# The gate rows of the second PEER layer: a new layout for one operand, and ScalarE for every second group of the other

## The chip, the core and the metric

The kernel runs on one core of a Trainium2 chip. The metric is the device time of one execution in microseconds (us). A core has a matrix engine (TensorE, "PE" in the rows; its weight loads are "PEld"), three engines that work elementwise (VectorE "DVE", ScalarE "ACT", GpSimd "POOL"), and 16 DMA engines that are fed from queues, those of SyncE ("SPq") and GpSimd ("POOLq") here. Every engine takes its instructions in the order in which they stand in its queue; semaphores order engines among each other. That order was fixed when the program was built: a scheduler goes through the instructions in the order in which the code emits them, and lets a later instruction of an engine go ahead of an earlier one that by its own reckoning isn't ready yet.

## What is computed

Two layers of a trunk, each of a mixer and a PEER feed-forward. Only the second PEER (layer 1, no context output: 512 tokens, four tiles of 128) is touched:

```python
q = (hb @ w_q).reshape(PEER_BLOCK, PEER_HEADS, 2, half)
s = jnp.einsum('nhpd,pkd->nhpk', q, sub_keys)
sv, si = lax.top_k(s, PEER_TOPK)
...
top_s, pos = lax.top_k(cand, PEER_TOPK)      # 16 of the pairs (i, j) for each of 8 heads
gate = jax.nn.softmax(top_s, axis=-1)
act = gelu(einsum('nd,nhkd->nhk', hb, u_tab[eidx]))
w = gate * act
out = einsum('nhk,nhkd->nd', w, v_tab[eidx])
```

Each token picks 8 x 16 = 128 experts out of 128 x 128, an expert being a pair (i, j) with a gate.

## The kernel before

The second PEER is `peer_streams`. It treats its four token tiles in two ways. Two of them (`gath`) are gathered: for each of 128 slots of a tile an indirect DMA brings one row of 8 KB for each token (`gather`: POOL issues it, DVE multiplies and sums the first half against the token, ACT makes the gelu and the weight, DVE adds the second half into `acc`). Two tiles (`dense`, 256 tokens) go through all 16384 experts as matmuls: `u_pair` loads a pair of chunks of `u` (`u_raw`), multiplies it with the 256 tokens, takes the gelu, and keeps the result in a ring of 14 tiles in on-chip memory, or, when the ring is full, stores it to DRAM (`aw`, `A_d`) and loads it back later. Then 64 steps of a second loop load a pair of chunks of `v` (`v_raw`), multiply the activations with the gates (`gg`, on POOL, L1459) and accumulate `res` on TensorE; a step also makes a `u_pair` if any is left, or reloads one from `A_d`.

The gates of the dense tiles must be spread over all experts first, and that is what `build` does: for a token, the 128 x 128 matrix of gates is the product of two matrices whose rows are the token's 128 picks, one with a one at column i (`o1`), one with the gate at column j (`o2`). `tr` holds i (negated), j and the gate with the picks on partitions and the tokens along the free axis; `ib` and `jb` are i and j in bfloat16. A group is W8 = 4 tokens: DVE makes `o1` (compare a counting row with i, L1273), `oe` (compare with j, L1275; the counting row is repeated four times, tokens innermost, which is also how `oe` is laid out) and `o2` (`oe` times the gate, L1276). `o2` is stored token by token, so L1276 walks its output with a stride of 128 elements, and each of the four matmuls (L1281, recorded at the helper's line L73) reads 128 elements that lie side by side. ACT copies the product into `stage` (L1283), and after 16 tokens a DMA stores the stage to `G_d`. Each tile has 32 groups, so there are 64 in all. `o1` and `o2` have two buffers each, `oe` one. In the trace `o1` and `o2` are both called `o`. A float32 matmul is recorded as two passes, so a group is eight records of 128 columns.

The first PEER (`peer`, layer 0) builds its gates by another function of its own, lines 818 to 840: `o1` by ACT (four Abs, L829, and one Relu, L830), `o2` by DVE.

What is emitted when is set by a planner written into the kernel. `fill` is called after each piece of TensorE's work with that work's time. It advances a clock for TensorE and emits pieces of other work until DVE's clock has caught up: pieces of `choice` (selection of the experts of a tile, and `build` of the tile before, in turns), and gather slots, one unit of slot time for three of `choice` (FRONT_SHARE). The times are those of the table PAY. While `choice` lasts, each turn also emits a `u_pair`; when it is used up, the pools of this stage close, and the loop over `v` follows. The slots left over are emitted along that loop and at its end.

Of the kernel before, what the change touches and what calls it, by code (L numbers as in the profile page):

```python
# [9 lines left out]
F32 = mybir.dt.float32  # L10
# [4 lines left out]
AF = mybir.ActivationFunctionType  # L15
OP = mybir.AluOpType
# [64 lines left out]
def kernel(tc, a, out):  # L81
    nc = tc.nc
    V, S, G, PE, SP = nc.vector, nc.scalar, nc.gpsimd, Tracked(nc.tensor), nc.sync
# [7 lines left out]
    def pool(stack, name, bufs=1, space=None, side="left"):  # L91
        return stack.enter_context(tc.tile_pool(name=name, bufs=bufs, space=space, reuse_waits="tile") if space
                                   else tc.tile_pool(name=name, bufs=bufs, side=side, reuse_waits="tile"))
# [9 lines left out]
    def kt(shape, name, dt=F32):  # L103
        return kp.tile(shape, dt, name=name)
# [19 lines left out]
    iota, row = kt([P, P], "iota"), kt([P, 1], "row")  # L124
# [1002 lines left out]
    def peer_streams(op, l, gt, xdst):  # L1127
# [4 lines left out]
        n, nr = nd * P, (nd + ng - 1) * P  # L1132
# [10 lines left out]
        wp = pool(ef, "ps_f")  # L1143
# [3 lines left out]
        iotab = wp.tile([P, P], BF16, name="iotab")  # L1147
# [109 lines left out]
        W8, W4 = 4, 4  # L1257
# [3 lines left out]
        def build(t):  # L1261

            tr, ib, jb = chosen.pop(t)
            for g in range(P // TG):
                stg = wp.tile([P, P, TG], F32, name="stage", bufs=2)
                for b in range(TG // W8):
                    n0 = g * TG + b * W8
                    nb = slice(n0, n0 + W8)
                    sh, hs = [P, W8, P], [P, P, W8]
                    o1 = wp.tile(sh, F32, name="o1", bufs=2)  # L1270
                    oe = wp.tile(hs, BF16, name="oe", bufs=1)
                    o2 = wp.tile(sh, F32, name="o2", bufs=2)
                    V.tensor_tensor(o1, iotab.unsqueeze(1).to_broadcast(sh), ib[:, nb].unsqueeze(2).to_broadcast(sh),  # L1273
                                    op=OP.is_equal)
                    V.tensor_tensor(oe, iotar, jb[:, nb].unsqueeze(1).to_broadcast(hs), op=OP.is_equal)  # L1275
                    V.tensor_tensor(o2.rearrange("p n c -> p c n"), oe, tr[:, 2, nb].unsqueeze(1).to_broadcast(hs),  # L1276
                                    op=OP.mult)
                    for i4 in range(0, W8, W4):
                        pq = pp.tile([P, W4, P], F32, name="gps", tag="misc", bufs=4)
                        for i in range(W4):  # L1280
                            PE.matmul(pq[:, i], o1[:, i4 + i], o2[:, i4 + i], start=True, stop=True)  # L1281
                        n1 = b * W8 + i4
                        S.copy(stg[:, :, n1:n1 + W4].rearrange("p i n -> p n i"), pq)  # L1283
                        yield "build"
                tg = (dense.index(t) * P) // TG + g
                SP.dma_start(G_d[:, :, tg], stg.rearrange("p (q c) m -> p q (c m)", c=GG))

        def gather(i):
# [23 lines left out]
            for args in late:  # L1312
# [1 line left out]

        clock = {"pe": 0.0, "dve": 0.0, "dma": 0.0}
        PAY = {"score": (1.75, 0, .25), "cand": (.6, 0, 0), "top": (.85, 0, 0), "top2": (.55, 0, 0), "decode": (1.0, 0, 0),
               "eq": (1.4, 0, 0), "tree": (1.05, 0, 0), "gates": (1.0, 0, .6), "build": (1.9, .65, .9),
               "slot": (2.75, 2.5, 0)}

        def pay(kind):  # L1320
# [12 lines left out]
        def choice():  # L1333
            yield from select(dense[0])
            for t, u in zip(dense, [*dense[1:], gath[1]]):
                gens = [build(t), select(u)]
                while gens:
                    for q in list(gens):
                        kind = next(q, None)
                        if kind is None:  # L1340
                            gens.remove(q)
                        else:
                            yield kind
# [103 lines left out]
        for j in range(NP):  # L1447
            c = 2 * j
# [561 lines left out]
    with ExitStack() as es:  # L2010
        gt = gather_state(0, es)
        op = mixer0(gt)
        nxt = peer(op, 0, gt, x_d[1])
    with ExitStack() as es:
        gt = gather_state(1, es)
        op = mixer1(*nxt, gt)
        peer_streams(op, 1, gt, out.rearrange("(t p) d -> t p d", p=P))
# [76 lines left out]
```

## Time and profile before

| | us |
|---|---|
| median of 3 runs | 3853.35 |
| lowest and highest of the runs | 3850.56, 3860.54 |
| the profiled execution, its own time | 3857.99 |
| span of the profiled execution | 3856.2 |

A row of instructions gives line, engine, operation, output<-inputs, shapes and count, then busy time in us and mean ns of one, then the engine's idle time just before them and what ended it. A mean ns is the duration of one record; records of TensorE overlap, so its rate is busy time divided by count. [...] The profile's own table of busy shares over the whole span mixes this layer with the first one, and says little about it.

### The profile page before, as it was taken

Reading aid. Unit: us, or ns where it says so; the run is one execution under the profiler, and the core shown is the slowest. Engines: PE = TensorE matmul, PEld = TensorE weight load, DVE = VectorE, ACT = ScalarE, POOL = GpSimd, SP = SyncE. Lnnn points to the kernel's source line nnn. Section 1 sums busy time; section 2 is a strip of 40 time slices with the busy share of each in tenths; the row PEclk is TensorE's granted clock in tenths of the full one; section 3 lists DMA queues with packets and bytes.
Section 4 is the critical chain, followed back from the end, with each engine's and each line's share of the span. In section 5 each row is a group of like instructions: output and inputs, shape, how many; then the busy total and the mean of one; then the engine's idle time right before and its main releaser. Section 6 shows DMA issues by size and latency. Waiting matters only on the chain. (4 is left out here: it accounts for less than half of the span.)

```text
span 3856.2 us, 50097 instructions
## 1 busy us (share of the span) xinstructions
PE 3538.3 (92%) x17628; PEld 2749.2 (71%) x17628; DVE 3009.0 (78%) x6281; ACT 1409.0 (37%) x2760; POOL 1635.1 (42%) x1225
## 2 busy tenths in 40 slices
PE   7789999999999999999998999979998789898987
PEld 6567877788888778888887888755887336555643
DVE  4877899999999868988886616469999556766675
ACT  4243322378888933322224424312343111111110
POOL 3300055446444557888771203101123344545462
PEclk8899999999999999999999999899999899999988
DMA  5225588889999999999994330245699999999995
GB/s 231 88 85 191 178 325 308 308 313 358 359 346 351 372 333 358 361 365 356 364 339 147 127 126 4 98 144 197 229 331 409 398 400 411 413 421 421 421 421 223
DMA packets 331772, 1121.13 MB, mean 291 GB/s; under 512 B 28161, under 2 KB 136065, under 8 KB 261377
## 3 DMA queue, kind: packets, MB, share of 16 engines
q1 hardware_dynamic: 217616, 562.92, 39.2%
q0 software_dynamic: 113760, 554.75, 37.2%
q8 instruction: 139, 2.28, 0.2%
q14 instruction: 113, 0.92, 0.1%
q10 hardware_dynamic: 144, 0.26, 0.0%
HBM read 1021.88 MB, written 95.94 MB: 290 GB/s over the span
## 5 line engine op out<-in xcount | busy, mean ns | idle before, releaser
L1302 POOL DMA_INDIRECT g_row<-in_peer_uv_dram,g_idx x256 | 344.1, 1344 | 631.6 <-DVE g_acc L1298 375.8
L73 PE MATMUL res<-v_raw,w 128*128 128x512 f32 x1024 | 485.0, 632 | 105.8 <-DMA v_raw<-in_peer_v_dram 98.8
L691 POOL DMA_INDIRECT g_row<-in_peer_u_dram,g_idx x256 | 363.3, 1419 | 366.4 <-DVE g_row L695 136.1
L73 PE MATMUL ups<-opc,u_raw 128*128 128x256 f32 x2048 | 466.2, 385 | 11.7 <-DMA u_raw<-in_uT_dram 9.5
L73 PEld LDWEIGHTS res<-v_raw,w 128*128 128x128 f32 x1024 | 205.4, 203 | 365.5 <-issue 338.5
L691 POOL DMA_INDIRECT g_row<-in_peer_v_dram,g_idx x256 | 378.6, 1479 | 204.8 <-DVE g_acc L699 129.8
L73 PE MATMUL ups<-opah,c_hi 128*128 128x512 f32 x1152 | 459.0, 398 | 5.9 <-ACT c_hi L318 5.9
L73 PE MATMUL ups<-opah,c_lo 128*128 128x512 f32 x1152 | 453.7, 395 | 9.6 <-DVE c_lo L319 9.3
L1305 DVE SCALAR_TENSOR_TENSOR g_row<-g_row,g_h 128x1024 f32<-128x1024 f32 x256 | 326.2, 1274 | 168.7 <-DMA g_row<-in_peer_uv_dram,g_idx 168.5
L73 PEld LDWEIGHTS ups<-opc,u_raw 128*128 128x128 f32 x2048 | 393.7, 194 | 81.8 <-issue 17.2
L73 PE MATMUL ups<-opal,c_hi 128*128 128x512 f32 x1152 | 452.0, 392 | 0.0
L1298 DVE SCALAR_TENSOR_TENSOR g_acc<-g_row,g_w,g_acc 128x1024 f32<-128x1024 f32 x254 | 335.3, 1320 | 113.3 <-ACT g_w L1307 112.9
L699 DVE SCALAR_TENSOR_TENSOR g_acc<-g_row,g_act,g_acc 128x1024 f32<-128x1024 f32 x254 | 369.5, 1455 | 1.9
L695 DVE SCALAR_TENSOR_TENSOR g_row<-g_row,g_h 128x1024 f32<-128x1024 f32 x256 | 333.0, 1319 | 3.9 <-DMA g_row<-in_peer_u_dram,g_idx 3.9
L1306 ACT ACTIVATE g_d<-g_d 128x1 f32<-128x1 f32 x256 | 52.0, 203 | 775.7 <-DVE g_row L1305 775.7
L73 PE MATMUL res<-v_hi,w_hi 128*128 128x512 f32 x1024 | 316.8, 390 | 2.1 <-ACT w_hi L318 2.1
L73 PE MATMUL res<-v_hi,w_lo 128*128 128x512 f32 x1024 | 316.9, 390 | 0.0
L73 PE MATMUL res<-v_lo,w_hi 128*128 128x512 f32 x1024 | 316.5, 390 | 0.0
L318 ACT CAST c_hi<-c_raw 128x1024 fp32r<-128x1024 f32 x160 | 167.6, 1048 | 373.8 <-PE ups L73 281.6
L318 ACT CAST v_hi<-v_raw 128x1024 fp32r<-128x1024 f32 x128 | 134.9, 1054 | 423.4 <-PE res L73 304.3
L1083 POOL TENSOR_TENSOR w<-ag,gg 128x512 f32<-128x512 f32 x128 | 235.4, 1839 | 116.0 <-DVE w_lo L319 109.1
L319 DVE TENSOR_TENSOR v_lo<-v_raw,v_hi 128x1024 fp32r<-128x1024 f32 x128 | 180.8, 1413 | 106.3 <-ACT v_hi L318 106.3
(523 smaller groups left out, 6992.8 us busy)
## 6 DMA issues: line engine op xcount, KB each, us to landing
v_raw<-in_peer_v_dram SPq DMA_DIRECT2D x128, 1024.0 KB, 9.4
c_raw<-in_uT_dram SPq DMA_DIRECT2D x128, 512.0 KB, 6.7
u_raw<-in_uT_dram SPq DMA_DIRECT2D x64, 1024.0 KB, 10.6
G_d<-stage SPq DMA_DIRECT2D x48, 1024.0 KB, 9.4
gg<-G_d SPq DMA_DIRECT2D x64, 512.0 KB, 9.7
A_d<-at SPq DMA_DIRECT2D x120, 256.0 KB, 6.3
ag<-A_d SPq DMA_DIRECT2D x30, 1024.0 KB, 11.6
modw<-in_mod_w_dram SPq DMA_DIRECT2D x10, 2048.0 KB, 8.4
```

Source lines behind the costliest of these rows:

```text
L73: self.last = self.engine.matmul(*args, **kw)
L318: copied[0] = S.copy(hi, src)
L319: return V.tensor_tensor(lo, src, hi.bitcast(F32), op=OP.subtract)
L691: G.indirect_dma_start(out=row, out_offset=None, in_=a[f"peer_{'uv'[tab]}{l}"], in_offset=bass.IndirectOffsetOnAxis(ap=idx[i][:, s:s + 1], ...
L695: V.scalar_tensor_tensor(row, row, 1.0, h, op0=OP.mult, op1=OP.mult, accum_out=w)
L699: V.scalar_tensor_tensor(acc, row, w, acc, op0=OP.mult, op1=OP.add)
L1083: G.tensor_tensor(w.rearrange("p (t m) -> p t m", m=TG), ag[:, i], gg[:, :, (c + i) % GG, :], op=OP.mult)
L1298: V.scalar_tensor_tensor(acc, row[:, D:], w, acc, op0=OP.mult, op1=OP.add)
L1302: G.indirect_dma_start(out=row, out_offset=None, in_=a[f"peer_uv{l}"], in_offset=bass.IndirectOffsetOnAxis(ap=idx[i][:, s:s + 1], axis=0))
L1305: V.scalar_tensor_tensor(row[:, :D], row[:, :D], 1.0, h, op0=OP.mult, op1=OP.mult, accum_out=d)
L1306: S.activation(d, d, AF.Gelu)
```

## The change

`o2` is now laid out as `oe` is, with the four tokens innermost; DVE writes it in order, and a matmul reads its 128 columns four elements (16 bytes) apart. For every second group (even `b`) `o1` is made by ACT, as the first PEER does it: four Abs over 128 elements and one Relu over 512. In the planner's table a group's DVE time goes from 1.9 to 1.5.

```diff
-                    o2 = wp.tile(sh, F32, name="o2", bufs=2)
-                    V.tensor_tensor(o1, iotab.unsqueeze(1).to_broadcast(sh), ib[:, nb].unsqueeze(2).to_broadcast(sh),
-                                    op=OP.is_equal)
+                    o2 = wp.tile(hs, F32, name="o2", bufs=2)
+                    if b % 2:
+                        V.tensor_tensor(o1, iotab.unsqueeze(1).to_broadcast(sh),
+                                        ib[:, nb].unsqueeze(2).to_broadcast(sh), op=OP.is_equal)
+                    else:
+                        for i in range(W8):
+                            S.activation(o1[:, i], iota, AF.Abs, bias=tr[:, 0, n0 + i:n0 + i + 1])
+                        S.activation(o1, o1, AF.Relu, bias=1.0, scale=-1.0)
                     V.tensor_tensor(oe, iotar, jb[:, nb].unsqueeze(1).to_broadcast(hs), op=OP.is_equal)
-                    V.tensor_tensor(o2.rearrange("p n c -> p c n"), oe, tr[:, 2, nb].unsqueeze(1).to_broadcast(hs),
-                                    op=OP.mult)
+                    V.tensor_tensor(o2, oe, tr[:, 2, nb].unsqueeze(1).to_broadcast(hs), op=OP.mult)
...
-                            PE.matmul(pq[:, i], o1[:, i4 + i], o2[:, i4 + i], start=True, stop=True)
+                            PE.matmul(pq[:, i], o1[:, i4 + i], o2[:, :, i4 + i], start=True, stop=True)
...
-               "eq": (1.4, 0, 0), "tree": (1.05, 0, 0), "gates": (1.0, 0, .6), "build": (1.9, .65, .9),
+               "eq": (1.4, 0, 0), "tree": (1.05, 0, 0), "gates": (1.0, 0, .6), "build": (1.5, .65, .9),
```

## Rows read from the trace of the kernel before

**Rows 1.** First line of the profile's page.
```profile
span 3856.2 us, 50097 instructions
```

**Rows 2.** Stretches: us, busy PE, PEld, DVE, ACT, POOL, PEclk, DMA share, GB/s.
```profile
2735.00:2850.00 115.00, 106.33 (x567) 94.76 (x568) 111.92 (x312) 51.03 (x73) 15.17 (x10) 0.93 0.72 246
2850.00:3005.00 155.00, 138.51 (x748) 122.09 (x746) 148.75 (x214) 56.86 (x125) 52.92 (x36) 0.97 1.03 402
3005.00:3200.00 195.00, 148.89 (x332) 67.69 (x331) 103.19 (x119) 20.96 (x81) 86.34 (x77) 0.90 0.99 395
3200.00:3780.00 580.00, 517.92 (x1674) 324.89 (x1673) 398.27 (x466) 93.03 (x337) 309.02 (x232) 0.94 1.01 420
```

**Rows 3.** The first two stretches again, DVE's instructions of L1276 alone.
```profile
2735.00:2850.00 115.00, 29.24 (x28) 0.93 0.72 246
2850.00:3005.00 155.00, 36.56 (x35) 0.97 1.03 402
```

**Rows 4.** Groups of instructions by shape, 2733 to 2996 us.
```profile
L73 PE MATMUL gps<-o,o 128*128 128x128 f32 x512 | 67.7, 284 | 21.9 <-DVE o L1276 21.3 <-ACT stage L1283 0.3
L1276 DVE TENSOR_TENSOR o<-oe,ijT 128x512 f32<-128x512 bf16 x64 | 66.8, 1044 | 0.0
L1283 ACT COPY stage<-gps 128x512 f32<-128x512 f32 x64 | 64.0, 1049 | 43.7 <-PE gps L73 23.1 <-DMA G_d<-stage 20.7
L1298 DVE SCALAR_TENSOR_TENSOR g_acc<-g_row,g_w,g_acc 128x1024 f32<-128x1024 f32 x44 | 56.0, 1274 | 0.0
L1305 DVE SCALAR_TENSOR_TENSOR g_row<-g_row,g_h 128x1024 f32<-128x1024 f32 x43 | 52.4, 1219 | 0.5 <-DMA g_row<-in_peer_uv_dram,g_idx 0.4
L1273 DVE TENSOR_TENSOR o<-iotab,iT 128x512 f32<-128x512 bf16 x63 | 42.9, 681 | 6.9 <-PE gps L73 6.9
L1275 DVE TENSOR_TENSOR oe<-iotar,jT 128x512 bf16<-128x512 bf16 x64 | 26.5, 415 | 0.0
```

**Rows 5.** Waits, 2733 to 2996 us: who for whom, us, times, longest.
```profile
POOL g_row L1302 <- DVE g_acc L1298: 140.1, 39, 20.3
PE gps L73 <- DVE o L1276: 21.3, 13, 3.9
```

**Rows 6.** Chain that ended last, in order of time: start, us, what.
```profile
3004.48 12.75 DMA G_d<-stage
3017.80 8.71 DMA v_raw<-in_peer_v_dram
...
3795.55 36.30 PE res L73 x84
```

**Rows 7.** Groups by shape, whole run, TensorE: the matmuls of u_pair.
```profile
L73 PE MATMUL ups<-opc,u_raw 128*128 128x256 f32 x2048 | 466.2, 385 | 11.7 <-DMA u_raw<-in_uT_dram 9.5 <-ACT stage L1283 2.2
```

**Rows 8.** DMA issues, 2537 to 3856 us: count, KB each, us to landing.
```profile
u_raw<-in_uT_dram SPq DMA_DIRECT2D x61, 1024.0 KB, 10.7
A_d<-aw SPq DMA_DIRECT2D x14, 256.0 KB, 12.1
```

**Rows 9.** First PEER, 800 to 1345 us: ACT's groups, and gate matmuls waiting for them.
```profile
L829 ACT ACTIVATE o<-iota,ijT 128x128 f32<-128x128 f32 x512 | 167.6, 403 | 0.1
L830 ACT ACTIVATE o<-o 128x512 f32<-128x512 f32 x128 | 81.1, 633 | 1.9
  ACT o L830: 30.0, 39
```

**Rows 10.** Side by side and apart, whole run: groups by shape, then single lines (min/median/max ns).
```profile
L318 ACT CAST c_hi<-c_raw 128x1024 fp32r<-128x1024 f32 x160 | 167.6, 1048 | 373.8 <-PE ups L73 281.6 <-PE zps L73 43.5 <-issue 25.2
L233 ACT COPY pg<-gps 128x512 f32<-128x512 f32 x6 | 3.5, 586 | 7.3 <-PE gps L73 7.2
L319 DVE TENSOR_TENSOR c_lo<-c_raw,c_hi 128x1024 fp32r<-128x1024 f32 x160 | 196.1, 1227 | 77.1 <-ACT c_hi L318 77.0
L1228 DVE TENSOR_TENSOR ijg<-eq x16: 245/266/274, 2598.6 to 2848.6; 128x64 f32<-128x64 bf16 x16
L1210 DVE TENSOR_TENSOR ps<-pos,ps x8: 206/216/232, 2592.3 to 2835.9; 128x64 uint32<-128x64 uint32 x8
```

## The prediction, made before the changed kernel was run

> **What bounds the kernel now.** I read the stretches of the second PEER first, because the busy shares of the whole span mix two layers. From 3200 to 3780 us the 16 DMA engines are full (share 1.01) and move a flat 420 GB/s, while DVE is busy for 398 of 580 us [rows 2]. So the loop over `v` is a matter of bytes: a megabyte row set of a gather or a chunk pair of `u` or `v` costs 2.5 us there (1.049 MB at 420 GB/s), whichever engine asks for it. From 2850 to 3005 us the DMA engines are nearly as full, at 402 GB/s. Only in the first stretch, 2735 to 2850 us, do they have room: 246 GB/s [rows 2]. What holds them back there is DVE, busy for 111.9 of 115 us, and the waits say how: the gathers' issue on POOL waited 140.1 us for DVE to add up a row and give its buffer back [rows 5].
>
> TensorE is the second engine to watch. It is busy for 106.3 of 115 and 138.5 of 155 us [rows 2], and its wait before the gate matmuls is 21.3 us, for L1276 [rows 5]. The end of this stage matters because nothing of the loop over `v` starts before it: the last store of gates, 12.8 us, and then a first `v` load stand in the chain that ended last [rows 6]. The end of the program is 36 us of `res` matmuls on TensorE and a norm [rows 6], which the change doesn't touch.
>
> **DVE's part.** L1276 takes 1044 ns for 512 elements, L1273 takes 681 ns for as many, also float32 out of bfloat16, but written side by side [rows 4]. I take 681 for the new L1276 (bounds: 681 and 1044), which saves 64 x 0.363 = 23.2 us. L1273 falls away for 32 groups: 32 x 0.681 = 21.8 us. Together 45.0 us of DVE time; L1275 stays [rows 4].
>
> **ACT's part.** ACT gets 32 x (4 x 0.403 + 0.633) = 71.8 us from the first PEER's durations [rows 9]. It was busy for 51 + 57 of 270 us [rows 2], so it goes to about 180 and doesn't become the bound. Its queue is in order, though: ahead of the copies to `stage`, the gelus of `u_pair` and the two small steps of each slot there may now stand 2.2 us of Abs and Relu. The nearest row for what waits on this is the first PEER, where gate matmuls stood 30.0 us for L830 in 128 groups [rows 9]: 0.234 us each, 7.5 us for 32. Less than nothing it can't be, more than twice that would need DVE's slots to wait too; I take 7.5.
>
> **The planner's part.** Adding up PAY through `fill` by hand, `choice` is used up after 28 `u_pair` and 25 slots with 1.9 for a group, and after 23 and 22 with 1.5. (That the count is sound shows in the 14 stores to `A_d` [rows 8]: 28 less a ring of 14.) So five pairs move from this stage into the loop over `v`, with everything they issue: 5 x 1024 KB of `u_raw` on SP's queue [rows 8] and TensorE work of 466.2 / 64 = 7.28 us each [rows 7], which is 36.4 us that no longer stands ahead of the last gates. Five stores of 256 KB to `A_d` and their reloads fall away [rows 8]. The loop over `v` gets 5.24 - 1.31 = 3.93 MB more, 9.4 us at 420 GB/s.
>
> **TensorE's part: the read with a stride.** This is the disputed cost. A pass of 128 columns now takes 67.7 / 512 = 0.132 us [rows 4]; no row shows TensorE reading its 128 columns apart, so I bound it. Below: 0.132, no cost (a gain has no reason). For the other side there are three rows of what single elements far apart cost other engines. DVE's L1276 pays 0.71 ns an element more than L1273 for writing apart [rows 4]. ACT's copy to `stage` takes 1049 ns against 586 for 512 elements side by side, 0.90 ns an element more [rows 4, 10]. And reading: L1228, whose two inputs are read 16 elements apart, takes 266 ns for 64 elements against 216 for L1210, 0.78 ns more [rows 10]. With DVE's own pace, (1227 - 681) / 512 = 1.07 ns [rows 4, 10], a lone element takes 1.78 ns on DVE; with ACT's, (1048 - 586) / 512 = 0.90 [rows 10], 1.81 ns on ACT. Two engines of different pace end at the same 1.8 ns, which points to the memory and not to the engine. At 1.78 ns a pass takes 0.227 us, and 512 passes cost 48.6 us more. The upper end is ACT's whole time for an element apart, 1049 / 512 = 2.05 ns: 0.262 us, 66.6 us more. I take 0.227, since a row of reading agrees with it.
>
> [...]
>
> **The sum.** The stage up to the last gate matmul is DVE-bound before, with TensorE close behind. With the strided passes it is TensorE's: -36.4 (five pairs) + 48.6 (stride) - 21.3 (its wait for L1276, which DVE now meets early) + 7.5 (waits for ACT) = -1.6 us. DVE then has 45.0 - 1.6 = 43 us over. What it could do with them is slots, at 1.274 + 1.219 = 2.5 us each [rows 4], up to 17; each that is done ahead takes 2.5 us of transfer out of the loop over `v`. But DVE's queue is in order, groups stand in it ahead of later slots, and with two buffers for `o2` DVE stands behind TensorE. I take 4 slots, -10.0 us (bounds 0 and -43). With the loop's +9.4 the total is -2.2 us. From the profiled execution's 3857.99 (1.8 us of it outside the span of 3856.2 [rows 1]) that gives 3855.8; that execution stands 4.6 us above the median of the runs, so against the median: **3851 us**, no change. This case's own range, with 0 to 9 slots and a pass of 0.20 to 0.24 us, is 3836 to 3867.
>
> **The rivals.** A: TensorE reads with that stride for nothing. Then TensorE's limit falls by 36.4 + 21.3 - 7.5 = 50.2 us and DVE's by 45.0, so the stage follows DVE. Of 63 groups 28 lie in the stretch with room on the DMA engines [rows 3], which shortens by 28/63 x 45.0 = 20.0 us. The later stretch moved 155 x 0.402 = 62.3 MB [rows 2]; less 35/63 of the 6.55 MB that the five pairs took, that is 58.7 MB, and at 420 GB/s no less than 139.7 us: 15.3 us saved. With the loop's +9.4 this is -25.9 us, **3827**; if slots are put off rather than waited for, -45.0 + 9.4 = -35.6, 3818. For it: a pass of 128 columns isn't at the matmul's own pace (128 columns at the 0.89 ns of `u_pair`, 7.28 us / 32 / 256 [rows 7], would be 0.114 us), so some of a slower read is hidden. Against it: the three rows above.
>
> B, slower: TensorE's strided pass goes at 2.05 ns a column, the whole pace of ACT's copy. Then the stage is 16.4 us longer (-36.4 + 66.6 - 21.3 + 7.5), DVE stands behind it and does no slot ahead, and the loop's 9.4 us come on top: +25.8, **3879**. It decides from a pass of 0.234 us on (52.4 us over 512 passes), where the total goes over +11.6. For it: five pairs have only been moved, TensorE has them still to do in a loop where it is busy for 518 of 580 us [rows 2].
>
> C: the change doesn't make L1276 faster, because its 1044 ns come from the gate operand and not from the output's stride. Then DVE saves 21.8 us only; with a free stride that is -21.8 + 9.4 = -12.4, **3841**. L1273, the only row as near, has two bfloat16 operands, so it isn't excluded.
>
> **How the numbers follow.** Chances: the forecast 0.48, A 0.31, B 0.16, C 0.05. A measurement of this kernel can tell about 0.3%, 11.6 us, from no change. Faster by more: A, half of C and a fifth of the forecast's case, 0.44. Slower by more: B and a tenth of the forecast's case, 0.22 with rounding. Within: 0.34. The range goes from A's lower value, 3818, to just short of B's, 3877, which leaves out the ends of A and B, some 0.17.
>
> **What would show it.** Busy time over count of the gate matmuls is the first thing to read: 0.13 is A, 0.23 the forecast, 0.26 B. L1276 near 681 ns or 1044 decides C. The number of `aw` stores should fall from 14 to 9. ACT's Abs and Relu should take 0.40 and 0.63 us. In the forecast's case the last gate matmul stays near 2990 us and TensorE's wait for L1276 is gone; in A it comes 35 to 45 us earlier, and the stretch after 2735 us moves well over 246 GB/s. The prediction fails if the scheduler puts slots ahead where I let DVE stand, which would take the forecast's case down towards A, or if ACT's new work makes the slots late, which would show as waits of DVE for the weight `g_w` before 3005 us.

## The result, and the profile after

| | us |
|---|---|
| before, median of 6 runs (lowest to highest) | 3853.70 (3850.56 to 3860.54) |
| after, median of 6 runs (lowest to highest) | 3875.16 (3871.85 to 3882.45) |
| ratio, with its 95% interval | 1.0054 (1.0041 to 1.0068) |
| profiled execution of after, and its span | 3874.32, 3872.5 |

The change makes the kernel 0.54% slower. The prediction said 3851 us, no change: that is wrong. The time lies inside its range, close to the rival B (3879), whose sign and size it has; that B hits by luck is said further down.

First the same stretches as in [rows 2], of the kernel after (us, busy PE, PEld, DVE, ACT, POOL, the granted clock of TensorE as a share of its full speed, the mean busy share of the 16 DMA engines, GB/s):

```profile
2735.00:2850.00 115.00, 114.67 (x517) 101.24 (x516) 94.76 (x284) 74.68 (x146) 12.03 (x9) 1.00 0.66 225
2850.00:3005.00 155.00, 142.86 (x629) 124.76 (x628) 121.22 (x180) 76.83 (x187) 40.78 (x30) 0.97 1.00 362
3005.00:3200.00 195.00, 165.40 (x442) 87.47 (x443) 102.44 (x119) 22.55 (x86) 88.80 (x81) 0.92 0.99 406
3200.00:3780.00 580.00, 510.15 (x1668) 322.57 (x1668) 405.74 (x473) 95.60 (x345) 315.08 (x228) 0.95 1.01 421
```

In the first stretch the two engines have changed places: TensorE is busy for 114.67 of 115 us, DVE for 94.76 (111.92 before). The DMA engines, which had room before, move less than they did: 225 GB/s, not 246.

The groups by shape from 2700 to 3010 us, which answer [rows 4], say what TensorE is busy with:

```profile
L73 PE MATMUL gps<-o,o 128*128 128x128 f32 x512 | 124.3, 406 | 8.6 <-DVE o L1281 3.9 <-ACT o L1279 3.8
L1281 DVE TENSOR_TENSOR o<-oe,ijT 128x512 f32<-128x512 bf16 x64 | 44.0, 687 | 12.2 <-PE gps L73 12.2
L1278 ACT ACTIVATE o<-iota,ijT 128x128 f32<-128x128 f32 x128 | 42.0, 393 | 0.0
L1274 DVE TENSOR_TENSOR o<-iotab,iT 128x512 f32<-128x512 bf16 x32 | 22.2, 692 | 36.1 <-PE gps L73 35.9
L1279 ACT ACTIVATE o<-o 128x512 f32<-128x512 f32 x32 | 20.2, 630 | 0.6
```

L1276 of before is L1281 now, L1273 is L1274. The gate matmuls take 124.3 us instead of 67.7: 0.243 us a pass, not 0.132. DVE's two steps are what the change meant them to be: 1044 ns have become 687, and half of the comparisons are gone. But in the last column DVE now stands for 35.9 + 12.2 = 48 us behind the gate matmuls, for a buffer of `o1` or `o2` to come free. The 45 us that it saved are spent in waiting for TensorE.

What the gate matmuls (PE) and their weight loads (PEld) waited for (us, times, longest), and the end of the chain that ended last (start, us):

```profile
PE gps L73 <- DVE o L1281: 3.9, 1, 3.9
PE gps L73 <- ACT o L1279: 3.8, 2, 2.3
PEld gps L73 <- ACT o L1279: 13.6, 13, 4.3
```
```profile
3777.32 7.12 PE res L73 x16
3784.45 11.27 DMA v_raw<-in_peer_v_dram
3795.86 52.42 PE res L73 x116
```

The two engines' waits must not be added up: weight loads run beside the matmuls (in the 289.2 us up to the last gate matmul, PE is busy for 280.6 and PEld for 247.2), so what TensorE loses is the line of PE. The view of one tile does add them (17.4 us here), and so does the line of [rows 9]: of its 30.0 us, 10.8 are waits of matmuls and 19.2 of weight loads.

The last line of the chain is the one to set beside [rows 6]. In both kernels the chain's last wait is over by about 3796 us: before it was for a product of gates on POOL, after for a load of `v`. Then TensorE has 84 `res` matmuls left before and 116 after: 36.3 and 52.4 us. These 16.1 us are as much as the difference of the two profiled executions (3874.32 - 3857.99 = 16.3), but they don't explain it: e3_plan below has a loop as long as after's and ends in 36.30 us again, and e13_plan11, with a loop 39.8 us longer than after's, ends in 24.29.

To see where the time comes from I cut the time by TensorE's own events: from the first `u_pair` of the layer to the last gate matmul (the front), from there to the first `res` (the gap), and to the last `res` (the loop over `v`). Before, then after, same columns:

```profile
2698.00:2991.30 293.30, 266.26 (x1421) 235.31 (x1419) 285.93 (x664) 114.07 (x208) 71.51 (x48) 0.96 0.87 323
2991.30:3026.60 35.30, 19.79 (x74) 16.22 (x74) 21.43 (x26) 6.50 (x21) 8.47 (x9) 0.82 1.04 388
3026.60:3837.00 810.40, 713.57 (x2102) 410.23 (x2102) 511.43 (x594) 116.71 (x424) 402.60 (x317) 0.94 0.97 399
```
```profile
2689.70:2978.90 289.20, 280.61 (x1263) 247.23 (x1262) 240.25 (x617) 165.57 (x355) 56.83 (x42) 0.99 0.82 291
2978.90:3010.80 31.90, 18.32 (x74) 14.90 (x73) 19.47 (x23) 4.65 (x17) 8.83 (x8) 0.81 0.93 351
3010.80:3853.40 842.60, 744.50 (x2262) 439.76 (x2262) 527.23 (x612) 121.91 (x441) 415.17 (x323) 0.94 0.96 396
```

The front became 4.1 us shorter, the gap 3.4 us, and the loop 32.2 us longer: 24.7 in all. (The layer began 8.3 us earlier in this execution of after, ahead of anything that the change touches; 24.7 - 8.3 gives the 16.4 at the end. In the runs below the layer begins between 2685.5 and 2700.4 us, so I compare lengths within the layer.) TensorE's idle time is length less busy time: 27.0, 15.5 and 96.8 us before, 8.6, 13.6 and 98.1 after. In the loop it has hardly moved: 30.9 of the 32.2 us are work, 160 more matmul records of the five `u_pair`s that were moved there.

### The profile page after: what moved, and what is told of

Read it like the earlier page. It is cut to its first block, busy times and chain, and to the rows that moved or that the text cites. A ratio compares the mean times of both kernels' runs of the same rounds, so it can differ in the third digit from the quotient of the medians.

```text
span 3872.5 us, 50238 instructions
## 1 busy us (share of the span) xinstructions
PE 3573.2 (92%) x17628; PEld 2780.7 (72%) x17628; DVE 2984.3 (77%) x6249; ACT 1463.6 (38%) x2920; POOL 1631.5 (42%) x1225
## 5 line engine op out<-in xcount | busy, mean ns | idle before, releaser
L1083 POOL TENSOR_TENSOR w<-ag,gg 128x512 f32<-128x512 f32 x128 | 226.6, 1771 | 112.9 <-DVE w_lo L319 105.8
L73 PE MATMUL gps<-o,o 128*128 128x128 f32 x1536 | 255.4, 320 | 19.5 <-ACT o L830 10.8
## 6 DMA issues: line engine op xcount, KB each, us to landing
u_raw<-in_uT_dram SPq DMA_DIRECT2D x64, 1024.0 KB, 10.7
```

Of the source, the lines that this page charges most:

```text
L73: self.last = self.engine.matmul(*args, **kw)
L1083: G.tensor_tensor(w.rearrange("p (t m) -> p t m", m=TG), ag[:, i], gg[:, :, (c + i) % GG, :], op=OP.mult)
```

## The experiments

Four theories, each tied to one part of the change. **The read** (S): TensorE pays for columns 16 bytes apart, and that is the loss. **The planner** (P): the five pairs that 1.5 instead of 1.9 moves into the loop cost there what they save ahead of it, or more. **ACT's queue** (Q): Abs and Relu come late and hold the gates up. **DVE** (D; all letters are those of the expectations): DVE bounds the front, so whatever relieves it shortens the kernel by as much. The runs do one part alone, all but one, or put another layout in place of the strided one. Ratios are against the kernel before in the same series; they differ from the quotient of the two medians by up to 0.11%. Lengths and idle times are of one profiled execution each. In one table, for all runs that are told below, length and idle time of TensorE in us, cut as above:

| kernel | ratio (95%) | front, idle | gap, idle | loop, idle | total |
|---|---|---|---|---|---|
| before | 1 | 293.3, 27.0 | 35.3, 15.5 | 810.4, 96.8 | 1139.0 |
| after | 1.0054 (1.0041 to 1.0068) | 289.2, 8.6 | 31.9, 13.6 | 842.6, 98.1 | 1163.7 |
| e1_layout | 1.0042 (1.0030 to 1.0055) | 316.1, 3.6 | 28.8, 12.9 | 812.1, 104.6 | 1157.0 |
| e2_act | 1.0017 (1.0004 to 1.0030) | 305.8, 36.7 | 35.0, 15.2 | 805.6, 94.9 | 1146.4 |
| e3_plan | 0.9971 (0.9959 to 0.9982) | 256.2, 23.8 | 30.6, 13.8 | 842.6, 97.6 | 1129.4 |
| e4_read | 0.9984 (0.9970 to 0.9999) | 262.1, 32.1 | 30.5, 14.4 | 840.6, 97.2 | 1133.2 |
| e5_pairs | 0.9993 (0.9983 to 1.0002) | 265.4, 34.3 | 29.9, 13.7 | 841.0, 94.4 | 1136.3 |
| e7_no_plan | 1.0041 (1.0028 to 1.0055) | 320.2, 5.3 | 32.6, 14.2 | 807.2, 91.5 | 1160.0 |
| e8_pairs_only | 0.9990 (0.9980 to 0.9999) | 286.5, 21.5 | 31.1, 15.3 | 811.0, 94.7 | 1128.6 |
| e9_pairs_plan | 0.9960 (0.9946 to 0.9973) | 238.6, 14.2 | 37.4, 19.4 | 845.1, 103.7 | 1121.1 |
| e10_stage3 | 0.9972 (0.9962 to 0.9982) | 258.2, 26.5 | 34.3, 15.2 | 845.2, 93.3 | 1137.7 |
| e12_best | 0.9950 (0.9936 to 0.9964) | 236.3, 12.1 | 39.6, 21.2 | 853.7, 110.6 | 1129.6 |
| e13_plan11 | 0.9931 (0.9918 to 0.9945) | 204.8, 10.6 | 28.9, 11.9 | 882.4, 101.4 | 1116.1 |
| e14_plan07 | 0.9951 (0.9938 to 0.9963) | 180.4, 11.9 | 27.9, 10.2 | 909.4, 104.2 | 1117.7 |

The column of the loop falls into steps by the number of pairs: 28 ahead of the gates give 806 to 812 us, 23 give 841 to 854, 18 give 882, 14 give 909.

### The layout alone

The kernel before, with these three lines of the change:

```diff
+                    o2 = wp.tile(hs, F32, name="o2", bufs=2)
+                    V.tensor_tensor(o2, oe, tr[:, 2, nb].unsqueeze(1).to_broadcast(hs), op=OP.mult)
+                            PE.matmul(pq[:, i], o1[:, i4 + i], o2[:, :, i4 + i], start=True, stop=True)
```

> The new layout of o2 alone: DVE writes it in order, TensorE reads 128 columns 16 bytes apart; no ScalarE part, planner's figure 1.9. Theory S (the strided read is what costs): the gate passes take 0.243 us as in the changed kernel (0.132 before), TensorE's work up to the last gate goes from 28 x 7.28 + 67.7 = 272 us to 328 us, less the 21 us it waited for L1276: the last gates 30 to 35 us later, 3875 to 3895 us in all. Theory P (the five pairs moved by the planner cost the time, at TensorE's 7.28 us each): no pairs move here, DVE saves 23 us, so 3840 to 3855 us.

Measured: 3872.03 against 3853.89 us, 1.0042, just below the range of theory S and far from that of P. The gate matmuls by shape:

```profile
L73 PE MATMUL gps<-o,o 128*128 128x128 f32 x512 | 122.6, 404 | 3.5 <-DVE o L1276 3.5
```

0.239 us a pass. The front is 316.1 us long and TensorE idle in it for 3.6: it is TensorE's alone. DVE's L1273 stands for 42.9 us behind gate matmuls. So this part alone gives three quarters of the loss (0.42 of 0.54%), although it takes 23 us off DVE.

### ACT's part alone

The kernel before, with:

```diff
+                    if b % 2:
+                        V.tensor_tensor(o1, iotab.unsqueeze(1).to_broadcast(sh),
+                                        ib[:, nb].unsqueeze(2).to_broadcast(sh), op=OP.is_equal)
+                    else:
+                        for i in range(W8):
+                            S.activation(o1[:, i], iota, AF.Abs, bias=tr[:, 0, n0 + i:n0 + i + 1])
+                        S.activation(o1, o1, AF.Relu, bias=1.0, scale=-1.0)
```

> ScalarE's part alone: Abs and Relu for every second group, old layout of o2, planner's figure 1.9. Theories S and P alike: DVE saves 32 x 0.681 = 21.8 us where it is the bound, ScalarE's 72 us stay beside: 3835 to 3850 us. Theory Q (ScalarE's queue: gates and slots wait behind Abs and Relu): 3860 us or more, with waits for the Relu of over 20 us.

Measured: 3864.19 us, 1.0017 (1.0004 to 1.0030), which is theory Q. It takes 22 us of comparisons off DVE, and the kernel gets slower, if by little. What the gate matmuls and ACT's copies to `stage` waited for (us, times, longest):

```profile
PE gps L73 <- ACT o L1279: 16.4, 9, 4.0
```
```profile
ACT stage L1288 <- DMA G_d<-stage: 31.9, 5, 9.3
```

ACT isn't full (busy for 167.8 of 305.8 us in the front). Its queue stands at a copy to `stage`, which waits for a store of gates to give the stage back, and the Abs and Relu of the next group are queued behind the copy. e10_stage3 tests that.

### The planner's number alone

The kernel before, with:

```diff
-               "eq": (1.4, 0, 0), "tree": (1.05, 0, 0), "gates": (1.0, 0, .6), "build": (1.9, .65, .9),
+               "eq": (1.4, 0, 0), "tree": (1.05, 0, 0), "gates": (1.0, 0, .6), "build": (1.5, .65, .9),
```

> The planner's figure alone, 1.5 for 1.9; the gate instructions are those of the kernel before. 23 pairs instead of 28 ahead of the last gates. Theory P: the five pairs cost the loop over v 5 x 7.28 = 36 us and the stage before gives back at most half of that, since DVE holds it: 3865 to 3880 us. Theory S: the planner's figure is harmless, 3845 to 3860 us.

Measured: 3847.05 us, 0.9971 (0.9959 to 0.9982): faster by 0.29% (6.8 us, or 0.18%, by the medians), as theory S had it and not P. Its three stretches:

```profile
2700.40:2956.60 256.20, 232.44 (x1262) 204.54 (x1261) 253.91 (x624) 107.66 (x179) 50.86 (x34) 0.96 0.82 292
2956.60:2987.20 30.60, 16.76 (x74) 14.26 (x74) 20.60 (x24) 4.76 (x17) 7.69 (x9) 0.83 1.02 402
2987.20:3829.80 842.60, 744.95 (x2262) 439.54 (x2262) 547.06 (x636) 126.11 (x457) 429.49 (x331) 0.94 0.98 406
```

The front gives up 37.1 us for five pairs, 7.4 each, and the loop gets 32.2, 6.4 each; TensorE's idle time in the loop stays (97.6). That a pair is a little cheaper in the loop, and the gap 4.7 us shorter, is the small gain; why, no run here shows.

This run also says which bytes count in the loop. In the kernel after, the loop moves 842.6 x 0.396 = 333.7 MB against 810.4 x 0.399 = 323.3 before: 10.3 MB more, 26 us at 399 GB/s, which would explain most of the 32.2. In e3_plan it moves 842.6 x 0.406 = 342.1 MB, 8.4 MB more again, and is as long to a tenth of a microsecond. The 8.4 MB are eight gathers. The DMA issues up to the last gate matmul, of after and of e3_plan (count, us to landing):

```profile
g_row<-in_peer_uv_dram,g_idx POOLq DMA_INDIRECT x54, 8.6
```
```profile
g_row<-in_peer_uv_dram,g_idx POOLq DMA_INDIRECT x46
```

Before, it is 60. So a gather put off costs the loop nothing here. The room for it is at the end: behind the last `u_pair`, in the last 120 us, the DMA share is 0.77 before, 0.68 after and 0.83 in e3_plan. Over all runs it isn't quite nothing: with 28 pairs, eight gathers more ahead of the gates (e2_act and e7_no_plan) go with a loop 5 us shorter, 0.6 us each, a quarter of the predicted 2.5. With 23 pairs the loops scatter too much to tell (841 to 854 us).

What a pair costs the loop is measured, then: 6.4 us. That it is TensorE's work that costs, and not the pair's own load beside the loads of `v`, is argued. For it: TensorE has 31.4 us more work in the longer loop, its idle time there is the same within 1 us, and its wait for `v_raw` hasn't grown (96.2 us in e3_plan, 98.8 before). Against it: up to the last `u_pair` the DMA engines are full in all three kernels (1.01 in the 600 us before it), so a load added there may hold up others. No run moved a pair's bytes without its work.

### The change with a read of adjacent elements

The kernel after, with:

```diff
-                            PE.matmul(pq[:, i], o1[:, i4 + i], o2[:, :, i4 + i], start=True, stop=True)
+                            PE.matmul(pq[:, i], o1[:, i4 + i], o2.rearrange("p c n -> p (c n)")[:, (i4 + i) * P:(i4 + i + 1) * P], start=True, stop=True)
```

The 128 neighbours belong to four tokens, so this kernel leaves out the sorting by token and its gates don't hold; its instructions and transfers are those of the change.

> The changed kernel, except that each gate matmul reads 128 elements of o2 that lie side by side (the wrong 128: the gates' product is left wrong; all instructions, waits and transfers stay). Theory S: passes back at 0.132 us, and the time is that of the rival with a free stride, 3818 to 3836 us. Theory P: the moved pairs still cost the loop over v, 3850 to 3865 us.

Measured: 3849.41 us, 0.9984 (0.9970 to 0.9999). Everything of the change is there except the stride of the read. The passes are back at the old pace, as theory S says (0.136 us); the time is a little below theory P's 3850 to 3865 and far above S's 3818 to 3836. The gate matmuls by shape, and what they and their weight loads waited for:

```profile
L73 PE MATMUL gps<-o,o 128*128 128x128 f32 x512 | 69.8, 288 | 32.0 <-ACT o L1279 25.0 <-DVE o L1281 3.9 <-DVE oe L1280 3.2
```
```profile
PE gps L73 <- ACT o L1279: 25.0, 13, 11.3
PEld gps L73 <- ACT o L1279: 37.6, 15, 11.5
```

The read costs 3875.16 - 3849.41 = 25.8 us (0.70% by the two ratios). It is the loss: without it the change wins 4.5 us by the medians, 6 by the ratio. But it isn't the whole story. The passes became 54.5 us cheaper and the front only 27.1 us shorter, because TensorE's idle time in it rose by 23.5 us: its matmuls now wait 25.0 us for ACT where they waited 3.8. The slow read had covered ACT's lateness. (The 63 us for ACT that the expectations below name are matmuls and weight loads added up.)

### The tokens in twos: written in order, read 8 bytes apart

`oe` and `o2` are laid out as two pairs of tokens, each 128 columns by 2, so that DVE still writes in order (its row of `o2` is 683 ns) and a matmul reads every second element. The lines that choose the token pair for the two DVE steps are left out here.

```diff
-                    sh, hs = [P, W8, P], [P, P, W8]
+                    sh, hs = [P, W8, P], [P, W8 // 2, P, 2]
...
-                            PE.matmul(pq[:, i], o1[:, i4 + i], o2[:, :, i4 + i], start=True, stop=True)
+                            PE.matmul(pq[:, i], o1[:, i4 + i], o2[:, (i4 + i) // 2, :, i % 2], start=True, stop=True)
```

With the rest of the change:

> The changed kernel with o2 laid out in twos: two tokens innermost, so DVE still writes in order and TensorE's columns lie 8 bytes apart, two to 16 bytes. Theory L (what costs is that each column needs 16 bytes of its own): passes back at 0.132 us, L1281's successor at 0.69 us, and the time of the run that read side by side, 3842 to 3857 us. Theory M (any read apart costs): passes at 0.24 us, 3865 to 3880 us.

And alone, with ACT's part and the planner's number undone:

> The layout in twos alone: no ScalarE part, planner's figure 1.9. DVE saves 23 us as in the run with the new layout alone. Theory T (TensorE's work and its idle time make the total; DVE counts only through TensorE's wait for o2, 21 to 27 us before the last gates): with passes at 0.132 us 3835 to 3850 us. Theory D (DVE's time is the bound there, each microsecond of it counts): 3825 to 3835 us. If 8 bytes cost as 16 do: 3865 to 3880 us.

Measured: e5_pairs 3849.55 against 3853.19 us, 0.9993 (0.9983 to 1.0002); e8_pairs_only 3846.88, 0.9990 (0.9980 to 0.9999). The gate matmuls of the one and of the other:

```profile
L73 PE MATMUL gps<-o,o 128*128 128x128 f32 x512 | 71.2, 288 | 34.2 <-ACT o L1279 27.2 <-DVE o L1283 3.9 <-DVE oe L1282 3.1
```
```profile
L73 PE MATMUL gps<-o,o 128*128 128x128 f32 x512 | 66.7, 279 | 9.2 <-DVE o L1278 8.3 <-ACT g_w L1308 0.6
```

0.139 and 0.130 us a pass: 8 bytes apart costs TensorE nothing (in order it is 0.132 before [rows 4], 0.136 in e4_read, 0.140 in e2_act), and e5_pairs has the time of e4_read. So the times are those of theory L; why 16 bytes cost and 8 don't, no run shows. What e8_pairs_only gains is the more telling number. DVE has lost 23 us of work and TensorE nothing, and the front became 6.8 us shorter, the median 6.3 (4 us by the ratio). With DVE as the bound of the front it would have been some 20: theory D falls. TensorE is busy for 265 of 286.5 us in that front. Its wait for `o2` fell by 13 us, from 21.3 [rows 5] to 8.3, and half of that went into a wait for loads of `u`, which was 4.9 us before:

```profile
PE ups L73 <- DMA u_raw<-in_uT_dram: 12.3, 3, 5.0
```

### The change without the planner's number

The kernel after, with:

```diff
-               "eq": (1.4, 0, 0), "tree": (1.05, 0, 0), "gates": (1.0, 0, .6), "build": (1.5, .65, .9),
+               "eq": (1.4, 0, 0), "tree": (1.05, 0, 0), "gates": (1.0, 0, .6), "build": (1.9, .65, .9),
```

> The changed kernel with the planner's figure back at 1.9: new layout with the 16-byte read and ScalarE's part. If the parts add up (layout +18, ScalarE +10, planner -7 us against the kernel before), 3880 to 3888 us. If ScalarE's part costs nothing while TensorE is slowed by the read (its waits for the Relu were 17 us in the changed kernel, 63 us with the read side by side), 3870 to 3879 us.

Measured: 3870.41 against 3854.56 us, 1.0041 (1.0028 to 1.0055): the second case. It is e1_layout with ACT's part added, and has e1_layout's ratio, though ACT's part alone cost 0.17%. The gate matmuls waited 0.9 us for ACT here, 16.4 in e2_act. The parts don't add up: where the read makes TensorE late, ACT is in time. And the planner's number, worth -0.29% alone, is worth nothing on top of the strided read (1.0041 and 1.0054): the front gets 31.0 us shorter, the loop 35.4 longer.

### Twos and the planner's number, ACT's part undone; and a third stage

e9_pairs_plan is e5_pairs with all comparisons on DVE, as before. e10_stage3 is e5_pairs with a third buffer for `stage` and, to make room, one tile less in the ring; its edit is shown. `stage` shares its buffers with `q_raw`, the loads ahead of the layer's first `u_pair`, which so get a third one too. e12_best has both.

```diff
-RING = 14
+RING = 13
...
-                stg = wp.tile([P, P, TG], F32, name="stage", bufs=2)
+                stg = wp.tile([P, P, TG], F32, name="stage", bufs=3)
...
-                held[0] = wp.tile([P, 2, KB, P], F32, name="q_raw", tag="stage", bufs=2)
+                held[0] = wp.tile([P, 2, KB, P], F32, name="q_raw", tag="stage", bufs=3)
```

> The layout in twos and the planner's figure 1.5, no ScalarE part. Theory T: the planner's 7 us and what is left of TensorE's wait for o2, 23 us there: 3820 to 3842 us, and faster than the changed kernel with twos, because no gate waits for ScalarE. Theory D: ScalarE's part saves DVE 22 us, so leaving it out costs: slower than the changed kernel with twos.

> The changed kernel with twos and a third buffer for stage (the ring of activations is one shorter for it, 13: one store and one reload of 256 KB more, 1.2 us). Theory W (gate matmuls wait for ScalarE because its queue stands at a copy to stage whose buffer a DMA still empties, 25 us in the run that read side by side): those waits go, the gates' wait for ScalarE falls from 63 us to under 35, 8 to 20 us faster than with two buffers. Theory O (they wait because Abs and Relu stand in order behind copies that need the matmuls before): under 5 us of difference.

> Layout in twos, planner's figure 1.5, no ScalarE part, a third buffer for stage and a ring of 13. Theory W: the 36 us for which ScalarE's copies stood for the stores of gates go, but without Abs and Relu behind them little of TensorE's time hung on that (7 to 14 us of waits for ScalarE): 3824 to 3838 us. If the buffer gained by itself and not through Abs and Relu, 3826 to 3832 us, as much faster than with two buffers as in the kernel with ScalarE's part, 7 us.

Measured: e9_pairs_plan 3836.78 against 3853.19 us, 0.9960 (0.9946 to 0.9973). Beside e5_pairs that is 13 us won by giving DVE its 32 comparisons back, as theory T has it. In both, ACT's copies wait for a store, longer in e9_pairs_plan (36.1 us, 28.4 in e5_pairs). But there no Abs and Relu stand behind them, and its front is 26.8 us shorter.

e10_stage3 takes that wait away: 3842.83 us, 0.9972, 6.7 us better than e5_pairs, between the two theories. What the gate matmuls waited for, in e5_pairs and in e10_stage3:

```profile
PE gps L73 <- ACT o L1279: 27.2, 13, 11.1
```
```profile
PE gps L73 <- ACT o L1279: 14.2, 13, 2.8
```

The wait of the copies for a store is gone, and half of the matmuls' wait for ACT with it. So the store is the cause of that half. What makes the other half stays open; the longest wait in ACT's queue there is that of the slots' small steps for DVE (`g_d`, 91.1 us), and no run takes it away. Where the 6.7 us sit stays open too: in the profiled executions the front is 7.2 us shorter, but gap and loop are 8.6 longer together, and the layer begins 10.7 us earlier (2685.5 against 2696.2). So the third buffer of `q_raw`, ahead of the layer, isn't excluded as their cause.

e12_best: 3835.92 us, 0.9950 (0.9936 to 0.9964), no more than e9_pairs_plan within the intervals. With no Abs and Relu behind the copies, the third buffer shows no gain.

### Further along the planner's number

e9_pairs_plan with the entry at 1.1 (18 pairs ahead of the gates; shown) and at 0.7 (14):

```diff
-               "eq": (1.4, 0, 0), "tree": (1.05, 0, 0), "gates": (1.0, 0, .6), "build": (1.5, .65, .9),
+               "eq": (1.4, 0, 0), "tree": (1.05, 0, 0), "gates": (1.0, 0, .6), "build": (1.1, .65, .9),
```

> Layout in twos, no ScalarE part, planner's figure 1.1: by its table fewer pairs still ahead of the last gates. Theory T (a pair costs TensorE the same on either side): the loop over v longer by 6 to 7 us a pair, the stage before shorter by as much as DVE allows: 3832 to 3845 us. If fewer pairs ahead of the gates are a gain by themselves, another 5 us or more: 3822 to 3832 us.

> Layout in twos, no ScalarE part, planner's figure 0.7: 14 pairs ahead of the last gates by its table, none stored to DRAM and reloaded (4 with 1.1, 9 with 1.5). Theory T: TensorE's work is the same on either side of the last gates and its idle time there is down to 10 us with 1.1, so nothing is left to gain: 3824 to 3834 us. If fewer pairs ahead of the gates go on gaining as from 1.5 to 1.1, 8 us or more: under 3822 us.

Measured: 3828.16 against 3854.56 us, 0.9931 (0.9918 to 0.9945), and 3834.90 against 3853.45, 0.9951 (0.9938 to 0.9963). e13_plan11 beats both kernels, by 0.69% and 1.2%, which theory T didn't expect; the last four pairs give some of it back, and e14_plan07 lies just above theory T's range. The chain's last line in the one and in the other:

```profile
3780.72 24.29 PE res L73 x52
```
```profile
3792.38 15.70 PE res L73 x36
```

This is the 36.3 us of [rows 6], and it shrinks: pairs and put-off gathers fill the DMA engines' time up to nearly the end (413 GB/s over the loop in e14_plan07, 399 before), so TensorE has less left after its last wait. That the loop now begins to be a matter of bytes would explain why e14_plan07 falls behind. It is argued from these lines only; no run took bytes away there.

## Why the prediction was wrong

Its terms, beside what the traces of before and after show. The front, gap and loop are those above; the miss is 24.7 - (-2.2) = 26.9 us within the layer (23.7 by the medians).

| term | predicted | shown |
|---|---|---|
| `u_pair` matmuls ahead of the last gates, five pairs fewer | -36.4 | -40.1 (207.8 to 167.7) |
| strided read, busy time | +48.6 | +56.6 (124.3 - 67.7) |
| wait for L1276 | -21.3 | -17.4 (3.9 left) |
| wait for ACT | +7.5 | +3.8 |
| wait for `u_raw` (4.9 before), and the rest | 0 | -7.0 |
| front together | -1.6 | -4.1 |
| gap | 0 | -3.4 |
| loop, five pairs | +9.4 | +32.2 (e3_plan too) |
| loop, slots done ahead | -10.0 | about 0 |
| total | -2.2 | +24.7 |

**What held.** The new L1276 takes 687 ns (681 predicted), so rival C falls. ACT's Abs and Relu take 393 and 630 ns. 23 pairs are ahead of the gates, and the stores of `aw` fall from 14 to 9:

```profile
A_d<-aw SPq DMA_DIRECT2D x9, 256.0 KB, 11.7
```

The slow read is real and TensorE bounds the front with it. The front's length came out within 2.5 us, though its terms were off by up to 8 in both directions: that is luck.

**The term that was mis-sized: the pass.** 0.243 us instead of 0.227, from the bounds 0.132 and 0.262. That is 8 us on busy time, and past the 0.234 from which rival B was to decide. It came from other engines' rows [rows 4, 10]: those gave the right kind of answer, and a slightly low one.

**The step that failed: "So the loop over `v` is a matter of bytes".** This is 22.8 of the 26.9 us: five pairs were priced at 9.4 us in the loop and cost 32.2. The prediction took the DMA share of 1.01 from 3200 to 3780 us [rows 2] for the bound, and priced the five pairs in the loop by 3.93 MB. Its own rows held a warning. The chain ends in 36.3 us of `res` without a wait [rows 6], so the end stood for TensorE and not for a transfer. And rival B's case had the very sentence: the pairs have only been moved, to where TensorE is busy for 518 of 580 us. At TensorE's price, 7.28 us each [rows 7], the term would have been +36.4 and the sum about +25. The runs show 6.4 us for a pair, near TensorE's price and far from the 1.9 us (9.4 / 5) of its bytes, while gathers cost next to nothing. That the price is TensorE's work, and not the pair's load in a full queue, is argued only, as said at e3_plan.

**The other step that failed: four slots done ahead, -10.0.** Their number had the wrong sign: 60 gathers are issued by the last gate matmul before, 54 after. The planner's 1.5 takes 14 away (46 in e3_plan), and ACT's part gives eight back (68 in e2_act, where the planner still has 1.9). It is 54 in e4_read and e5_pairs too, where DVE stands for only 16 us behind the gate matmuls, so the order of the program sets the number and not the time that DVE has over. And their price was next to nothing, as the eight gathers of e3_plan showed.

**The premise behind both: DVE bounds the front** (111.9 of 115 us busy, 140.1 us of gather waits behind it). DVE was full because the planner fills it with slots, as many as its table has room for; POOL's waits for `g_acc` say that gathers queue for DVE, not that the end waits for gathers. What was to be won at the front's end was TensorE's idle time in it, 27.0 us. e8_pairs_only measures it: 23 us less DVE, 6 us less time.

**ACT.** Its row was taken from the first PEER [rows 9] and read as waits of matmuls. Those are 10.8 of its 30.0 us, 0.084 us a group, 2.7 us for 32. Measured are 3.8 us under the slow read and 25.0 without it (e4_read), in a layer whose ACT queue holds copies that wait for stores. The sign that the prediction named for ACT's lateness, DVE waiting for `g_w`, didn't come under the slow read (0.6 us), but it did without it (11.9 us in e4_read).

**The rivals A and B.** e4_read is A's case, a free read, and took 3849 us, not 3827. A's stage came nearly out: 35.3 us shorter by its sum, 31.2 in the trace. What failed is again the loop, +9.4 against +30.2. B's number is near the result by luck: its front was to be 16.4 us longer and was 4.1 shorter, its loop 9.4 longer and was 32.2 longer.

## What to carry to other kernels

The layout of a tile has two prices, the writer's and the reader's (here DVE went from 1044 to 687 ns a step, TensorE from 0.132 to 0.243 us a pass); look for one that both can take (tokens in twos: 683 ns and 0.139 us in e5_pairs) before trading the one for the other. An engine that a planner keeps full with work that could be done later need not be the bound, however busy it is (DVE for 111.92 of 115 us, and 23 us less of its work were worth 6 us in e8_pairs_only): ask whose idle time the end would give back. Price work that is moved into another stage by every engine that it uses there, not only by the one that looks full. New work in an engine's queue inherits the waits of whatever stands ahead of it, so read what the instructions already there wait for. In the kernel before, ACT is idle for 10.81 us, until 2936.19 us, ahead of a copy to `stage` that waits for a store. The small step of a slot whose row DVE had finished at 2930.7 begins behind that copy, at 2937.04. And read waits by engine: a sum over matmuls and weight loads can exceed all the idle time that TensorE has (in e4_read 25.0 + 37.6 = 62.6 us of waits for ACT, against 32.1 us idle in the front).

## What the runs showed of the hardware

- A float32 matmul pass over 128 columns takes 0.132 to 0.140 us with the columns side by side (before, e2_act, e4_read), 0.130 to 0.139 us at 8 bytes apart (e5_pairs, e8_pairs_only), and 0.239 to 0.243 us at 16 bytes apart (e1_layout, e7_no_plan, after): 1.90 ns a column at the last. No run read at 12 bytes.
- That 1.90 ns lies beside DVE's 1.78 ns for a lone element and ACT's 1.81 [rows 4, 10], estimates that the prediction worked out from those rows. Three engines of different pace agree within 7%; why, no run here shows.
